# A hybrid decoder layer: the DeltaNet inverse with diagonal blocks of 32 instead of 16, solved on VectorE in groups of four steps

## The chip, the cores and the metric

One Trainium2 chip, one core. The metric is the device time of one execution in microseconds (us). TensorE (PE) multiplies matrices, VectorE (DVE), ScalarE (ACT) and GpSimd (POOL) work element by element, and SyncE (SP) issues the DMA transfers. Each engine runs its own instructions in the order in which the program emits them.

## The reference

One layer of a hybrid decoder on 16 learned meta tokens, 1024 prompt tokens and 8 sample sequences of 8 tokens. One projection of the normalised input (2048 wide) gives the columns of 6 mLSTM heads (A), 6 gated DeltaNet heads (B) and 4 HGRN2 heads (C), each 128 wide, and an output projection follows. The change is in the DeltaNet heads:

```python
def _gdn_segment(q, k, v, g, beta, S0, chunk):
    ...
    A = jnp.where(strict, bc[..., None] * decay * jnp.einsum('nbhtd,nbhsd->nbhts', kc, kc), 0.0)
    M = A + jnp.eye(c, dtype=A.dtype)
    rhs = jnp.concatenate([bc[..., None] * vc, (bc * jnp.exp(G))[..., None] * kc], axis=-1)
    sol = lax.linalg.triangular_solve(M, rhs, left_side=True, lower=True)
    ...
    def step(S, inp):
        q_, k_, U_, Wk_, Aqk_, G_ = inp
        W = U_ - jnp.einsum('bhtd,bhde->bhte', Wk_, S)
        o = jnp.exp(G_)[..., None] * jnp.einsum('bhtd,bhde->bhte', q_, S) + jnp.einsum('bhts,bhse->bhte', Aqk_, W)
        Ge = G_[..., -1:]
        S_new = jnp.exp(Ge)[..., None] * S + jnp.einsum('bhsd,bhse->bhde', k_ * jnp.exp(Ge - G_)[..., None], W)
        return S_new, o
```

In words: per chunk of tokens a unit lower triangular matrix M is inverted (the kernel forms the inverse and multiplies by it), and a state of 128x128 is carried from chunk to chunk.

## The kernel before

The tokens are handled in two halves of 512 prompt tokens; the first half also has the 64 sample and 16 meta tokens, a "small group" of `NT0` = 80. In each half the heads follow in the order gate, C0, B0, A0, B1, A1, C1, B2, A2, B3, A3, C2, B4, A4, B5, A5, C3. For each head `run_group` (line 303) does the projection: a weight block of 128x512 (`wraw`, by DMA) is split by ScalarE into a rounded part `whi` and by VectorE into the rest `wlo = wraw - whi`; three pieces are split ahead and seven loaded ahead. Each quarter of a piece gives three products into `acc` in the second half (`hB`: 512 columns) and six in the first (`hA`: two parts of 288 and 288 or 304 columns). After each quarter `weave.pump()` emits whatever else is due.

What else there is, is written as generators, the streams: the scan of a head (`gdn_scan` for B heads, with others for A and C), its finish, and others. Each stream runs to its next `yield` and gets a due time from a planner's own clock, `ck`: `ck.last + 0.4`, where `ck.last` is the time at which the planner thinks the emitted step is done, or what the code sets it to. A step is emitted when the planner's TensorE time `ck.t["T"]` has passed its due time. Within one queue the streams follow one another, so a scan that comes late makes the next scan late. This sets the order on all engines when the program is written; on the chip, semaphores only make an instruction wait for its operands.

`start_head` (line 1578) begins a head. If two heads are still live it drains the oldest: all its remaining steps are emitted at once, with no projection products between them:

```python
        while len(live) >= 2:
            weave.drain(*live.pop(0)["streams"]())
```

In `gdn_scan` the inverse of the 128x128 matrices of a half's four chunks (and of the small group) is built so. `B` (`Ball`) holds the strictly triangular parts. Diagonal blocks of `SUB` = 16 are solved in `substitute` by 15 steps of two VectorE instructions on `Yc` and `Yt`; each step needs a row of each block of `B` in all partitions of the block, which goes out to a DRAM scratch `db` and comes back broadcast as `Bb`. The result, masked to block diagonal, is `Y`; its transpose `X` is made by TensorE (`px`). Blocks of 16 are joined to 32 by full products `pz` and `pyy` with a mask `zmask` between; `X` is made anew; then blocks of 32 are joined to 64 and of 64 to 128 by small products of the same names. In these names of the trace, `s` and `t` stand for the shared tiles of the main and the small group (`Y`, `X`, `Z`, `vb` and others are such tiles).

Last, the chain of chunks, four rounds a head: `pr` (TensorE, old state `state_B` by keys), then VectorE on `vb` (`s<-pr`), then `pw` (TensorE, inverse by `vb`), ScalarE's copy `Wt`, then `pu` and two `po` (TensorE), VectorE's new `state_B`, and the next `pr`. There is a `yield` after each link, so that projection products can stand between.

The functions that the change touches, with their line numbers in the profile (most instructions are recorded at line 138, in a helper through which every operation goes):

Of the kernel before, what the change touches and what calls it, by code (L numbers as in the profile page):

```python
# [6 lines left out]
F32 = mybir.dt.float32  # L7
F32R = mybir.dt.float32r
U8 = mybir.dt.uint8
BF16 = mybir.dt.bfloat16  # L10
AF = mybir.ActivationFunctionType
ALU = mybir.AluOpType
AX = mybir.AxisListType

P = 128
# [176 lines left out]
def hybrid_step(ctx, tc, i, o):  # L192
    nc = tc.nc
    ck = Clock()
    V, S, G, T = (Engine(ck, n, e) for n, e in (("V", nc.vector), ("S", nc.scalar), ("G", nc.gpsimd), ("T", nc.tensor)))
    DMA = nc.sync.dma_start
    weave = Weave(ck)

    cp = ctx.enter_context(tc.tile_pool(name="cp", bufs=1))
# [24 lines left out]
    ident = cp.tile([P, P], F32, name="ident")  # L224
# [284 lines left out]
    segment_mask(sm0, 1.0, 0.0, True)  # L509

    hmask = {}
    zmask = cp.tile([P, P], BF16, name="zmask")
    m = sq("io", "zm")
    G.memset(m, 0.0)
    v = m.rearrange("p (b x) -> p b x", x=2 * SUB)[:, :, 0:SUB]
    G.memset(v, 1.0)
    G.affine_select(v, v, pattern=[[-2 * SUB, P // (2 * SUB)], [0, SUB]], compare_op=ALU.is_ge, fill=0.0, base=-SUB, channel_multiplier=1)
    G.affine_select(v, v, pattern=[[2 * SUB, P // (2 * SUB)], [0, SUB]], compare_op=ALU.is_ge, fill=0.0, base=2 * SUB - 1, channel_multiplier=-1)
    G.tensor_copy(zmask, m)
# [28 lines left out]
    for r in range(0, P, 32):  # L548
        v = quadmask[r:r + 32]
# [4 lines left out]
    for r in range(0, P, NSAMP):  # L554
        v = rowmask[r:r + NSAMP]
# [39 lines left out]
    rows_dram = [dp.tile([5, HA, h], F32, name=f"rows{h}") for h in (WA, WB)]  # L595
# [178 lines left out]
        return cols_of[half.index][0:g.n, g.idx, kind, h:h + 1].to_broadcast([g.n, g.nt, width])  # L774

    def bc_row(tag, name, half, arr, h):
        t = row(tag, name)[:, 0:half.width]
        DMA(t, rows_dram[half.index][arr, h:h + 1, :].partition_broadcast(P))
        return t


# [363 lines left out]
    def gdn_scan(half, h, ck_, cq, cv, zs, Gb, eG, bb, st):  # L1145
        W = half.width
        gs, main = half.ggroups, half.gmain
        cols = cols_of[half.index]
# [48 lines left out]
        for g, B in zip(gs, Bs):  # L1197
            n = g.n
# [7 lines left out]
        dbf = db.rearrange("j s c t -> j (s c t)")  # L1206
        Bb = []
        for lo, hi, tag in ((0, 6, "s7"), (6, 12, "s9"), (12, 15, "s6")):
            w = C * SUB
            t = sp.tile([P, 512], F32, tag=tag, name="Bb", bufs=1)[:, 0:(hi - lo) * w]  # L1210
            DMA(t, dbf[:, lo * w:hi * w].unsqueeze(1).to_broadcast([P // SUB, SUB, (hi - lo) * w]))
            for x in range(hi - lo):
                Bb.append(t[:, x * w:(x + 1) * w].rearrange("p (c t) -> p c t", t=SUB))
# [7 lines left out]
        Ys, Xs = [], []  # L1221

        def transpose_Y(g, Y, X):
            n = g.n
            px = bank("px")
            for c in range(g.nt):
                T.transpose(g.psum(px, n)[:, c], Y[0:n, c, 0:n], ident[0:n, 0:n])
            S.copy(X[0:n, :, 0:n], g.psum(px, n))

        def substitute():  # L1230
            Yc = sp.tile([P, 5, SUB], F32, tag="Yc", name="Yc", bufs=1)[:, 0:C]
            tmp = sp.tile([P, 5, SUB], F32, tag="Yt", name="Yt", bufs=1)[:, 0:C]
            V.tensor_copy(Yc, subid.unsqueeze(1).to_broadcast([P, C, SUB]))
            for s_ in range(SUB - 1):
                r = slice(s_ + 1, SUB)
                V.tensor_tensor(tmp[:, :, r], Yc[:, :, s_:s_ + 1].to_broadcast([P, C, SUB - 1 - s_]), Bb[s_][:, :, r], op=ALU.mult)
                V.tensor_tensor(Yc[:, :, r], Yc[:, :, r], tmp[:, :, r], op=ALU.subtract)
                if s_ in (4, 9):
                    ck.last = 0.0
                    yield  # L1240
            for g in gs:
                nb = g.n // SUB
                Y = gt("8", g)
                V.tensor_tensor(Y[0:g.n, :, 0:g.n].rearrange("p c (j t) -> p c j t", t=SUB),
                                Yc[0:g.n, g.idx].unsqueeze(2).to_broadcast([g.n, g.nt, nb, SUB]),
                                submask[0:g.n, 0:g.n].rearrange("p (j t) -> p j t", t=SUB).unsqueeze(1).to_broadcast([g.n, g.nt, nb, SUB]),
                                op=ALU.mult)
                Ys.append(Y)

# [83 lines left out]
        next(extra, None)  # L1333
        yield
        transpose_Y(main, Y, X)
        next(extra, None)
        yield
        for hh in (32, 64):
            pz = main.psum(bank("pz"))
            Z = gt("7", main)  # L1340
            blocks = [(slice(b, b + hh), slice(b + hh, b + 2 * hh)) for b in range(0, P, 2 * hh)]
            for l, r in blocks:
                for c in range(NC):
                    T.matmul(pz[r, c, 0:hh], B[l, c, r], X[l, c, l], start=True, stop=True)
            for l, r in blocks:
                S.copy(Z[r, :, 0:hh], pz[r, :, 0:hh])
            yield
            py = main.psum(bank("pyy"))
            for l, r in blocks:
                for c in range(NC):  # L1350
                    T.matmul(py[l, c, 0:hh], Z[r, c, 0:hh], Y[r, c, r], start=True, stop=True)
                    if hh == 32:
                        T.matmul(py[r, c, hh:2 * hh], Y[r, c, r], Z[r, c, 0:hh], start=True, stop=True)
            for l, r in blocks:
                V.tensor_scalar(Y[l, :, r], py[l, :, 0:hh], -1.0, None, op0=ALU.mult)
                if hh == 32:
# [309 lines left out]
    for half, groups in zip(halves, group_lists):  # L1666
# [4 lines left out]
        for n, group in enumerate(groups):  # L1671
# [14 lines left out]
            cols = [col for _, _, col in group]  # L1686
# [48 lines left out]
    for half in halves:  # L1735
        toks = []
        for n, (c0, cnt) in enumerate(half.tiles):
            if half.first and n == 0:
                toks.append((0, NSAMP, xs_flat, ys_flat))
            else:  # L1740
                a = HALF * half.index + c0
# [5 lines left out]
        for cg, some in OUT_UNITS[half.index]:  # L1747
# [28 lines left out]
            for n in some:  # L1776
                _, cnt, xsrc, _ = toks[n]
# [49 lines left out]
```

## Time and profile before

| what | value |
|---|---|
| three runs | 2525.36, 2528.02, 2525.58 us; median 2525.58 |
| the profiled execution | 2525.14 us, span of its instructions 2523.4 us |
| mean granted clock of TensorE | 0.992 |
| TensorE busy | 2456.8 us (97%) |
| VectorE busy | 1427.0 us (57%) |
| ScalarE busy | 1012.3 us (40%) |
| GpSimd busy | 555.0 us (22%) |
| DMA | 350.77 MB |

Rows of a timeline are: start, duration, engine, line, operation, output `<-` inputs, partitions x elements, number of instructions in the row, and in brackets how long the engine had been idle and what it waited for. `acc<-hB,wlo` is a projection product. PEld is the loading of weights into TensorE, beside the products. Rows of waits are: engine and tile, what it waited for, total us, times, longest. Rows of windows are: stretch in us from the start, its length, busy us of PE, PEld, DVE, ACT and POOL with the number of instructions, the granted clock, the DMA share and GB/s.

### The profile page before, as it was taken

What the parts mean: (1) busy time and instruction counts of PE and PEld (TensorE: products, weight loads), DVE (VectorE), ACT (ScalarE), POOL (GpSimd) and SP (SyncE); (2) the same over time, 40 slices, a digit from 0 to 9 for tenths busy, and PEclk for the clock granted to TensorE, in tenths of its full rate; (3) what the DMA queues carried; (4) which work ended last, traced back from release to release, by engine and by line L of the source; (5) the groups of instructions that cost most, each with busy time, mean ns of one, the idle gap of its engine ahead of it and who ended that gap; (6) DMA issues with size and microseconds to landing.
All of it is one profiled execution on the core that took longest, in us unless ns stands there. A gap on an engine that the chain in (4) does not pass through costs nothing.

```text
span 2523.4 us, 43205 instructions
## 1 busy us (share of the span) xinstructions
PE 2456.8 (97%) x15702; PEld 2199.6 (87%) x15702; DVE 1427.0 (57%) x2977; ACT 1012.3 (40%) x2476; POOL 555.0 (22%) x722
## 2 busy tenths in 40 slices
PE   6999999999999999999899999999999999999998
PEld 5899999999999999999687888888888888888886
DVE  7775656765746655556854556554554645323435
ACT  5643434343435333343643434333543334322324
POOL 5331211420314212213320103110320102211201
PEclk9999999999999999999999999999999999999999
DMA  5666655656545454448455445454554548636735
GB/s 129 157 143 147 154 135 122 166 135 133 144 97 143 97 128 115 118 105 225 115 134 122 119 121 130 120 132 100 131 128 111 130 118 264 175 83 195 259 96 184
DMA packets 681041, 350.77 MB, mean 139 GB/s; under 512 B 260004, under 2 KB 622076, under 8 KB 680828
## 3 DMA queue, kind: packets, MB, share of 16 engines
q1 hardware_dynamic: 680828, 348.01, 53.9%
q8 instruction: 123, 2.02, 0.3%
q14 instruction: 90, 0.74, 0.1%
HBM read 285.71 MB, written 62.19 MB: 138 GB/s over the span
## 4 chain that ended last, share of the span: by engine, by line
PE 74%; DMA 6%; issue 6%; DVE 5%; ACT 4%; POOL 3%; SPq 1%; POOLq 0%; DVEq 0%; ACTq 0%
PE acc L138 55%; PE oacc L138 8%; PE pa L138 1%; DVE wlo L138 1%; DMA wraw<-in_w_in_dram 1%; PE po L138 1%; POOL X L138 1%; PE pyy L138 1%; PE pz L138 1%; POOL res L138 1%; ACT whi L138 1%; PE pu L138 1%; ACT L138 1%; PE poh L138 1%; PE nd L138 1%
## 5 line engine op out<-in xcount | busy, mean ns | idle before, releaser
L138 DVE TENSOR_TENSOR wlo<-wraw,whi 128x512 fp32r<-128x512 f32 x720 | 528.4, 738 | 584.9 <-ACT whi L138 566.0
L138 PE MATMUL acc<-hA,whi 128*128 128x288 f32 (+1 forms) x4544 | 823.0, 303 | 11.5 <-ACT whi L138 7.0
L138 ACT CAST whi<-wraw 128x512 fp32r<-128x512 f32 x720 | 441.3, 618 | 879.8 <-PE acc L138 570.2
L138 PE MATMUL acc<-hB,whi 128*128 128x512 f32 x2272 | 723.8, 400 | 4.4 <-ACT whi L138 3.2
L138 PEld LDWEIGHTS acc<-hA,whi 128*128 128x128 f32 x4544 | 678.3, 191 | 17.5 <-ACT whi L138 8.4
L138 PE MATMUL acc<-hA,wlo 128*128 128x288 f32 x2240 | 488.9, 298 | 2.1 <-DVE wlo L138 2.0
L138 PEld LDWEIGHTS acc<-hB,whi 128*128 128x128 f32 x2272 | 411.2, 189 | 84.0 <-ACT whi L138 4.0
L138 PE MATMUL acc<-hB,wlo 128*128 128x512 f32 x1120 | 440.5, 393 | 5.1 <-DVE wlo L138 4.9
L138 PEld LDWEIGHTS acc<-hA,wlo 128*128 128x128 f32 x2240 | 367.1, 190 | 2.9 <-DVE wlo L138 2.9
L138 PE MATMUL oacc<-whi,y 128*128 128x512 f32 x1088 | 344.8, 391 | 1.7 <-ACT whi L138 1.6
L138 PEld LDWEIGHTS acc<-hB,wlo 128*128 128x128 f32 x1120 | 210.6, 188 | 55.9 <-DVE wlo L138 10.4
L138 PEld LDWEIGHTS oacc<-whi,y 128*128 128x128 f32 x1088 | 205.0, 188 | 45.6 <-ACT whi L138 3.4
L138 PE MATMUL oacc<-wlo,y 128*128 128x512 f32 x576 | 225.5, 392 | 2.1 <-DVE wlo L138 2.1
L138 PEld LDWEIGHTS oacc<-wlo,y 128*128 128x128 f32 x576 | 108.6, 189 | 26.1 <-DVE wlo L138 3.9
L138 POOL TENSOR_TENSOR res<-res,fnw 128x512 f32<-128x512 f32 (+1 forms) x34 | 54.3, 1624 | 255.3 <-ACT oscr L138 255.3
L138 POOL TENSOR_TENSOR qd<-qT,emb 128x512 f32<-128x512 f32 x12 | 16.8, 1403 | 355.9 <-PE po L138 355.9
L138 POOL TENSOR_TENSOR y<-y,zs 128x592 fp32r<-128x592 f32 (+1 forms) x32 | 45.5, 1420 | 92.4 <-ACT zs L138 62.8
L138 DVE TENSOR_TENSOR Yt<-Yc,Bb 128x60 f32<-128x60 f32 (+8 forms) x180 | 36.7, 204 | 39.4 <-DMA Bb<-db 34.4
L138 POOL TENSOR_TENSOR hr<-hr,halfneg 128x4 f32<-128x4 f32 (+1 forms) x48 | 47.4, 987 | 46.2 <-DVE hr L138 44.7
L138 POOL TENSOR_TENSOR X<-Ex,hk 128x256 f32<-128x256 f32 (+1 forms) x40 | 38.1, 953 | 87.8 <-PE pa L138 67.9
L138 POOL TENSOR_TENSOR nrm<-nrm,halfneg 128x10 f32<-128x10 f32 x12 | 23.5, 1955 | 122.6 <-DVE nrm L138 122.6
L138 DVE TENSOR_TENSOR Sx<-Sx,lf 128x256 f32<-128x256 f32 (+2 forms) x60 | 36.5, 613 | 20.2 <-ACT Ex L138 19.1
(410 smaller groups left out, 2805.8 us busy)
## 6 DMA issues: line engine op xcount, KB each, us to landing
wraw<-in_w_in_dram SPq DMA_DIRECT2D x564, 256.0 KB
wraw<-in_w_out_dram SPq DMA_DIRECT2D x144, 256.0 KB
y<-y SPq DMA_DIRECT2D x16, 576.0 KB
px<-in_x_prompt_dram SPq DMA_DIRECT2D x32, 256.0 KB
yd<-y SPq DMA_DIRECT2D x128, 64.0 KB
out_dram<-sst SPq DMA_DIRECT2D x16, 512.0 KB
s<-yd SPq DMA_DIRECT2D x32, 256.0 KB
y<-zs SPq DMA_DIRECT2D x32, 256.0 KB
```

The source lines that it names most:

```text
L138: return f(out, *a, **k)
```

## The change

`SUB` becomes 32. The solve takes 31 steps of two VectorE instructions, with a `yield` after every fourth step whose due time is `ck.t["T"] + 3.0` and 0.4; before, there were two `yield`s, due at once. The merge of 16 into 32 with its `zmask`, its `pz` and `pyy` and both `px` transposes go; the transposed blocks `Xc` come from a VectorE transpose of 32x32 blocks, and GpSimd clears `X` and copies two blocks of it. The rows of `B` are written to two scratches (full rows for the upper half of a block, half rows for the lower) and come back into tiles that are free by then: `ck_`, `Gb`, `bb` (rows `Ck`, `Gb`, `bb` in the order below), the old three, and in the first half `cv`. The first step is due 11 us instead of 7 us after the rows are sent for, and what follows the solve 7 us after it. `bc_row` hands out the whole row tile.

```diff
-SUB = 16
+SUB = 32
...
-        db = dp.tile([P // SUB, SUB, C, SUB], F32, name=f"db{half.index}{h}")
-        for j in range(P // SUB):
-            DMA(db[j], Ball[SUB * j:SUB * (j + 1), 0:C, SUB * j:SUB * (j + 1)])
+        nb = P // SUB
+        db = [dp.tile([nb, SUB // 2, C, w], F32, name=f"db{half.index}{h}{w}") for w in (SUB, SUB // 2)]
+        for j in range(nb):
+            a = SUB * j
+            DMA(db[0][j], Ball[a:a + SUB // 2, 0:C, a:a + SUB])
+            DMA(db[1][j], Ball[a + SUB // 2:a + SUB, 0:C, a + SUB // 2:a + SUB])
         Bb = []
-        for lo, hi, tag in ((0, 6, "s7"), (6, 12, "s9"), (12, 15, "s6")):
-            w = C * SUB
-            t = sp.tile([P, 512], F32, tag=tag, name="Bb", bufs=1)[:, 0:(hi - lo) * w]
-            DMA(t, dbf[:, lo * w:hi * w].unsqueeze(1).to_broadcast([P // SUB, SUB, (hi - lo) * w]))
...
-        ready = ck.t["T"] + 7.0
+        def spread_rows(t, cols):
+            at_ = 0
+            while len(Bb) < SUB - 1:
+                x, s_ = divmod(len(Bb), SUB // 2)
+                w = C * (SUB >> x)
+                m = min((cols - at_) // w, SUB // 2 - s_ - x)
+                if m == 0:
+                    return
+                src = db[x].rearrange("j s c t -> j (s c t)")[:, s_ * w:(s_ + m) * w]
+                DMA(t[:, at_:at_ + m * w], src.unsqueeze(1).to_broadcast([nb, SUB, m * w]))
...
+        for t in (ck_, Gb, bb):
+            spread_rows(t, UW)
+        for tag, cols_ in (("s7", 512), ("s9", 512), ("s6", 512), ("Bx", 320)):
+            if len(Bb) < SUB - 1:
+                spread_rows(sp.tile([P, cols_], F32, tag=tag, name="Bb", bufs=1), cols_)
+        ready = ck.t["T"] + 11.0
...
-                if s_ in (4, 9):
-                    ck.last = 0.0
+                if s_ % 4 == 3:
+                    ck.last = ck.t["T"] + 3.0
                     yield
+            V.transpose(Xc.rearrange("p c t -> p (c t)"), Yc[:, main.at:main.at + NC].rearrange("p c t -> p (c t)"))
...
+        spread_rows(cv, UW)
         ck.last = max(ck.last, ready)
         yield
         yield from substitute()
-        ck.last += 8.0
-        yield
-        Xs = [gt("9", main)]
-        transpose_Y(main, Ys[-1], Xs[-1])
+        ck.last = ck.t["T"] + 7.0
+        yield
         extra = first_chain() if half.first else iter(())
-        yield
-        B, Y, X = Bs[-1], Ys[-1], Xs[-1]
-        pz = main.psum(bank("pz"))
-        for c in range(NC):
-            T.matmul(pz[:, c], B[:, c], X[:, c], start=True, stop=True)
-        Z = gt("7", main)
-        V.tensor_tensor(Z, pz, zmask.unsqueeze(1).to_broadcast([P, NC, P]), op=ALU.mult)
-        next(extra, None)
-        yield
-        py = main.psum(bank("pyy"))
-        for c in range(NC):
-            T.matmul(py[:, c], Z[:, c], Y[:, c], start=True, stop=True)
-        V.tensor_tensor(Y, Y, py, op=ALU.subtract)
-        next(extra, None)
-        yield
-        transpose_Y(main, Y, X)
-        next(extra, None)
-        yield
-        for hh in (32, 64):
+        B, Y = Bs[-1], Ys[-1]
+        X = gt("9", main)[0:2 * SUB, :, 0:2 * SUB]
+        G.memset(X, 0.0)
+        for a in (0, SUB):
+            G.tensor_copy(X[a:a + SUB, :, a:a + SUB], Xc[a:a + SUB])
+        for hh in (SUB, 2 * SUB):
...
-                    if hh == 32:
-                        T.matmul(py[r, c, hh:2 * hh], Y[r, c, r], Z[r, c, 0:hh], start=True, stop=True)
+                    if l.stop == SUB:
+                        T.matmul(py[r, c, hh:2 * hh], y, Z[r, c, 0:hh], start=True, stop=True)
```

The later due times move the rest of each B scan. On TensorE, in the first chunk of the chain of head B3 in the second half, before:

```order
L138 MATMUL pr<-state_B_749,knT 128x128
L138 MATMUL acc<-hB_14887,whi 128x512
L138 MATMUL acc<-hB_14888,whi 128x512
L138 MATMUL acc<-hB_14887,wlo 128x512
L138 MATMUL acc<-hB_14676,whi 128x512
L138 MATMUL acc<-hB_14677,whi 128x512
L138 MATMUL acc<-hB_14676,wlo 128x512
L138 MATMUL pw<-s_20176,s_20233 128x128
```

and in the same place now:

```order
L137 MATMUL acc<-hB_14960,wlo 128x512
L137 MATMUL pr<-state_B_742,knT 128x128
L137 MATMUL pw<-s_20301,s_20625 128x128
L137 MATMUL pu_20773<-Wt,s_20183 128x128
L137 MATMUL po_20775<-state_B_742,qd 128x128
L137 MATMUL po_20775<-Wt,s_20282 128x128
L137 MATMUL pr<-state_B_742,knT 128x128
L137 MATMUL pw<-s_20301,s_20625 128x128
L137 MATMUL pu_20789<-Wt,s_20183 128x128
```

The products of projection that stood between `pr` and `pw` are gone from there; the links of this head's four chunks follow one another.

On VectorE, at the start of the solve of the same head, before:

```order
L138 TENSOR_TENSOR wlo<-wraw,whi 128x512
L138 TENSOR_TENSOR Yt<-Yc,Bb 128x4x15
L138 TENSOR_TENSOR Yc<-Yc,Yt 128x4x15
L138 TENSOR_TENSOR wlo<-wraw,whi 128x512
L138 TENSOR_TENSOR Yt<-Yc,Bb 128x4x14
L138 TENSOR_TENSOR Yc<-Yc,Yt 128x4x14
L138 TENSOR_TENSOR Yt<-Yc,Bb 128x4x13
```

and now, after the first group of four steps:

```order
L137 TENSOR_TENSOR Yc<-Yc,Yt 128x4x28
L137 TENSOR_TENSOR wlo<-wraw,whi 128x512
L137 TENSOR_TENSOR Yt<-Yc,Gb 128x4x27
L137 TENSOR_TENSOR Yc<-Yc,Yt 128x4x27
L137 TENSOR_TENSOR Yt<-Yc,Gb 128x4x26
L137 TENSOR_TENSOR Yc<-Yc,Yt 128x4x26
L137 TENSOR_TENSOR Yt<-Yc,Gb 128x4x25
L137 TENSOR_TENSOR Yc<-Yc,Yt 128x4x25
L137 TENSOR_TENSOR Yt<-Yc,Gb 128x4x24
L137 TENSOR_TENSOR Yc<-Yc,Yt 128x4x24
L137 TENSOR_TENSOR wlo<-wraw,whi 128x512
```

The steps are wider (4 chunks by up to 31 columns), and four of them stand between two weight pieces.

On TensorE, in the scan of the mLSTM head A1 in the first half, before:

```order
L138 MATMUL acc<-hA_88,wlo 128x304
L138 MATMUL pot<-ident,tho 80x128
L138 MATMUL pum<-meta_725,kwall 128x137
L138 MATMUL pum<-s_5279,kwall 128x129 x4
L138 MATMUL nd<-sst,spread_723 32x129 x8
L138 MATMUL nd<-t_5268,t_5218 32x129 x2
L138 MATMUL nd<-t_5268,t_5218 16x129
```

and now:

```order
L137 MATMUL pot<-ident,tho 80x128
L137 MATMUL pum<-meta_718,kwall 128x137
L137 MATMUL pum<-s_5436,kwall 128x129 x4
L137 MATMUL acc<-hA_82,whi 128x288
L137 MATMUL acc<-hA_82,whi 128x304
L137 MATMUL acc<-hA_83,whi 128x288
L137 MATMUL acc<-hA_83,whi 128x304
L137 MATMUL acc<-hA_82,wlo 128x288
L137 MATMUL acc<-hA_82,wlo 128x304
L137 MATMUL acc<-hA_84,whi 128x288
```

Twelve projection products now stand between `pum` and `nd`, where none did.

More of the change, by code (lines that the diff above doesn't have):

```diff
@@ L9 @@
 U8 = mybir.dt.uint8
-BF16 = mybir.dt.bfloat16
 AF = mybir.ActivationFunctionType
@@ L511, in hybrid_step @@
     hmask = {}
[L512 to L519, printed above, removed]
     submask = cp.tile([P, P], F32, name="submask")
@@ L776, in bc_row @@
     def bc_row(tag, name, half, arr, h):
-        t = row(tag, name)[:, 0:half.width]
-        DMA(t, rows_dram[half.index][arr, h:h + 1, :].partition_broadcast(P))
+        t = row(tag, name)
+        DMA(t[:, 0:half.width], rows_dram[half.index][arr, h:h + 1, :].partition_broadcast(P))
         return t
@@ L1202, in gdn_scan @@
             V.tensor_tensor(B[0:n, :, 0:n], B[0:n, :, 0:n], g.psum(pk, n), op=ALU.mult)
-        db = dp.tile([P // SUB, SUB, C, SUB], F32, name=f"db{half.index}{h}")
-        for j in range(P // SUB):
-            DMA(db[j], Ball[SUB * j:SUB * (j + 1), 0:C, SUB * j:SUB * (j + 1)])
-        dbf = db.rearrange("j s c t -> j (s c t)")
-        Bb = []
-        for lo, hi, tag in ((0, 6, "s7"), (6, 12, "s9"), (12, 15, "s6")):
-            w = C * SUB
-            t = sp.tile([P, 512], F32, tag=tag, name="Bb", bufs=1)[:, 0:(hi - lo) * w]
-            DMA(t, dbf[:, lo * w:hi * w].unsqueeze(1).to_broadcast([P // SUB, SUB, (hi - lo) * w]))
-            for x in range(hi - lo):
-                Bb.append(t[:, x * w:(x + 1) * w].rearrange("p (c t) -> p c t", t=SUB))
-        ready = ck.t["T"] + 7.0
+        nb = P // SUB
[4 more added lines that the diff above has]
+            DMA(db[1][j], Ball[a + SUB // 2:a + SUB, 0:C, a + SUB // 2:a + SUB])
+        Bb = []
+        def spread_rows(t, cols):
[8 more added lines that the diff above has]
+                DMA(t[:, at_:at_ + m * w], src.unsqueeze(1).to_broadcast([nb, SUB, m * w]))
+                for _ in range(m):
+                    Bb.append(t[:, at_:at_ + w].rearrange("p (c t) -> p c t", c=C))
+                    at_ += w
+        for t in (ck_, Gb, bb):
[4 more added lines that the diff above has]
+        ready = ck.t["T"] + 11.0
         if half.first:
@@ L1220, in gdn_scan @@
         yield
[L1221 to L1228, printed above, removed]
+        Ys = []
+        Yc = sp.tile([P, 5, SUB], F32, tag="Yc", name="Yc", bufs=1)[:, 0:C]
+        Xc = sp.tile([P, NC, SUB], F32, tag="Xc", name="Xc", bufs=1)
         def substitute():
-            Yc = sp.tile([P, 5, SUB], F32, tag="Yc", name="Yc", bufs=1)[:, 0:C]
             tmp = sp.tile([P, 5, SUB], F32, tag="Yt", name="Yt", bufs=1)[:, 0:C]
@@ L1343, in gdn_scan @@
                 for c in range(NC):
-                    T.matmul(pz[r, c, 0:hh], B[l, c, r], X[l, c, l], start=True, stop=True)
+                    T.matmul(pz[r, c, 0:hh], B[l, c, r], Xc[l, c] if hh == SUB else X[:, c], start=True, stop=True)
             for l, r in blocks:
                 S.copy(Z[r, :, 0:hh], pz[r, :, 0:hh])
+            next(extra, None)
             yield
@@ L1350, in gdn_scan @@
                 for c in range(NC):
-                    T.matmul(py[l, c, 0:hh], Z[r, c, 0:hh], Y[r, c, r], start=True, stop=True)
-                    if hh == 32:
-                        T.matmul(py[r, c, hh:2 * hh], Y[r, c, r], Z[r, c, 0:hh], start=True, stop=True)
+                    y = Yc[r, main.at + c] if hh == SUB else Y[r, c, r]
+                    T.matmul(py[l, c, 0:hh], Z[r, c, 0:hh], y, start=True, stop=True)
+                    if l.stop == SUB:
+                        T.matmul(py[r, c, hh:2 * hh], y, Z[r, c, 0:hh], start=True, stop=True)
             for l, r in blocks:
                 V.tensor_scalar(Y[l, :, r], py[l, :, 0:hh], -1.0, None, op0=ALU.mult)
-                if hh == 32:
+                if l.stop == SUB:
                     V.tensor_scalar(X[r, :, l], py[r, :, hh:2 * hh], -1.0, None, op0=ALU.mult)
```

9 lines of the change are left out of this document (5 added, 4 removed).

## The prediction

> **What bounds the kernel now.** I read the page first, then the list of waits, then the timeline of TensorE around the steps that the change touches.
>
> ```profile
> span 2523.4 us, 43205 instructions
> PE 2456.8 (97%) x15702; PEld 2199.6 (87%) x15702; DVE 1427.0 (57%) x2977; ACT 1012.3 (40%) x2476; POOL 555.0 (22%) x722
> ...
> q1 hardware_dynamic: 680828, 348.01, 53.9%
> ...
> PE 74%; DMA 6%; issue 6%; DVE 5%; ACT 4%; POOL 3%; SPq 1%; POOLq 0%; DVEq 0%; ACTq 0%
> ...
> L138 DVE TENSOR_TENSOR wlo<-wraw,whi 128x512 fp32r<-128x512 f32 x720 | 528.4, 738 | 584.9 <-ACT whi L138 566.0
> ...
> L138 ACT CAST whi<-wraw 128x512 fp32r<-128x512 f32 x720 | 441.3, 618 | 879.8 <-PE acc L138 570.2
> ```
>
> TensorE is busy 97% of the span and carries 74% of the chain. VectorE's idle time ends with ScalarE's `whi`, and ScalarE's ends with TensorE's `acc`: the two engines that prepare weight pieces wait for TensorE to use them up. So a microsecond that TensorE wins or loses counts in full, and work elsewhere costs only where it makes TensorE wait. The sum is made against the profiled execution of 2525.1 us, 0.5 us under the median of the three runs; I treat the two as equal.
>
> **Removed TensorE work.** Second half, head B3, TensorE around the merge of 16 into 32:
>
> ```profile
> 2038.75 0.40 PE L138 MATMUL acc<-hB,wlo 128*128 128x512 f32 x1
> 2038.98 1.05 PE L138 MATMUL pz<-s,Ball 128*128 128x128 f32 x8
> ...
> 2040.33 0.39 PE L138 MATMUL acc<-hB,wlo 128*128 128x512 f32 x1
> ...
> 2041.02 0.40 PE L138 MATMUL acc<-hB,wlo 128*128 128x512 f32 x1
> ...
> 2042.61 0.40 PE L138 MATMUL acc<-hB,wlo 128*128 128x512 f32 x1
> ...
> 2043.30 0.39 PE L138 MATMUL acc<-hB,wlo 128*128 128x512 f32 x1
> 2043.53 0.60 PE L138 MATMUL px<-ident,s 128*128 128x128 f32 x4
> ...
> 2044.43 0.39 PE L138 MATMUL acc<-hB,wlo 128*128 128x512 f32 x1
> ```
>
> The durations overlap, so I measure by period: three projection matmuls with nothing between, from `wlo` to `wlo`, take 0.69 us (2040.33 to 2041.02). With `pz` between it is 1.58, with `pyy` 1.59, with the four `px` transposes 1.13. They add 0.89, 0.90 and 0.44 us. The change drops `pz` and `pyy` once and `px` twice per head: 2.67 us, times 12 heads **−32 us**. The four narrow `pyy` matmuls that the merge of 32 loses count as nothing.
>
> **The chain of chunks loses its cover.** In the new order the scans of 11 of the 12 B heads (all but B5 of the second half) reach the drain in `start_head` with their chunk chains still to come, so `pr`, `pw`, `pu`, `po` stand there with no projection between (39 of 44 `pr`→`pw`, 42 `pw`→`pu`, 33 `po`→next `pr`). Before, each is spaced:
>
> ```profile
> 2058.33 0.39 PE L138 MATMUL acc<-hB,wlo 128*128 128x512 f32 x1
> ...
> 2058.56 0.38 PE L138 MATMUL pr<-state_B,knT 128*128 128x128 f32 x2
> ...
> 2058.98 0.35 DVE L138 SCALAR_TENSOR_TENSOR s<-pr,cols,s 128x128 f32<-128x128 f32 x1 [0.79 <-PE pr L138]
> ...
> 2059.25 0.40 PE L138 MATMUL acc<-hB,wlo 128*128 128x512 f32 x1
> ...
> 2059.48 0.40 PE L138 MATMUL pw<-s,s 128*128 128x128 f32 x2
> ...
> 2059.91 0.27 ACT L138 COPY Wt<-pw 128x128 f32<-128x128 f32 x1 [0.48 <-PE pw L138]
> ...
> 2060.18 0.40 PE L138 MATMUL acc<-hB,wlo 128*128 128x512 f32 x1
> ...
> 2060.87 0.40 PE L138 MATMUL acc<-hB,wlo 128*128 128x512 f32 x1
> ...
> 2061.11 0.38 PE L138 MATMUL pu<-Wt,s 128*128 128x128 f32 x2
> 2061.33 0.39 PE L138 MATMUL po<-state_B,qd 128*128 128x128 f32 x2
> ...
> 2061.75 0.35 DVE L138 SCALAR_TENSOR_TENSOR state_B<-state_B,eGb,pu 128x128 f32<-128x128 f32 x1 [1.60 <-PE po L138]
> ...
> 2062.24 0.39 PE L138 MATMUL acc<-hB,wlo 128*128 128x512 f32 x1
> ```
>
> Spaced, `pr` costs 0.92 − 0.69 = 0.23, `pw` 0.93 − 0.69 = 0.24, `pu` with both `po` 1.37 − 0.69 = 0.68: 1.15 us a chunk. Run together, TensorE waits out each link: from a matmul's start to its reader 0.42 or 0.43 us (2058.56→2058.98, 2059.48→2059.91, 2061.33→2061.75), then 0.35 in VectorE or 0.27 in ScalarE, then the way back. One place shows that and the start after a late weight load:
>
> ```profile
> 978.20 0.34 DVE L138 SCALAR_TENSOR_TENSOR state_B<-state_B,eGb,pu 128x128 f32<-128x128 f32 x1
> ...
> 978.60 0.30 PEld L138 LDWEIGHTS pr<-state_B,knT 128*128 128x128 f32 x2 [0.18 <-DVE state_B L138]
> ...
> 979.13 0.35 DVE L138 SCALAR_TENSOR_TENSOR s<-pr,cols,s 128x128 f32<-128x128 f32 x1 [0.58 <-PE pr L138]
> ```
>
> The way back is 0.06 (978.54→978.60), and a link whose weight load had to wait takes 0.53 from the load to the reader. So `pr`→`pw` is 0.53 + 0.35 + 0.06 = 0.94, `pw`→`pu` 0.53 + 0.27 + 0.06 = 0.86. From `pu` to the next `pr` VectorE also waits for the `po` that reads the old state: 0.22 (2061.11→2061.33), 0.42, 0.35 and 0.06, with 0.11 for the late load, 1.16. A chunk takes 2.96 us. Beyond the spaced cost the links are 0.71, 0.62 and 0.48, times 39, 42 and 33: **+70 us**, 6.3 a drain. The bounds: 0.97 us of VectorE and ScalarE plus three matmuls of 0.38 are 2.1 a chunk, +40 in all; half as much again as the sum is +105. I take the sum of links, since each piece of it is in a row of this very chain.
>
> In four of these drains (B1 and B3 of both halves) a C head's key activations stand between the `Wt` copies on ScalarE, elsewhere convolution steps on VectorE. A foreign instruction is of the size of a `whi` (0.62) or `wlo` (0.74). About 1.5 us in each of the four and 0.4 in the seven others: **+9** (0 to 20). The tail, where the last C head's products now follow each other with no projection left: **+4** (0 to 10), sized like four chunk links.
>
> **Relief of the mLSTM scans.** In the first half the drains of before fall on A scans:
>
> ```profile
> PE nd L138 <- DVE s L138: 4.8, 4, 1.8
> ...
> PE pum L138 <- ACT v L138: 2.0, 2, 1.0
> ...
> PE nd L138 <- DVE nsT L138: 1.6, 4, 1.1
> ```
>
> In the new order projection stands between these. The three waits sum to 8.4 us; with the unnamed pauses around them I take **−12** (−8 to −15).
>
> Without the clock: −32 + 70 + 9 + 4 − 12 = **+39**.
>
> **The granted clock.** One place before resembles the run-together chain: transposes, an eviction and products of a first-half B head.
>
> ```profile
> 198.00:204.00 6.00, 3.95 (x23) 3.23 (x22) 3.13 (x6) 3.48 (x10) 4.16 (x5) 0.80 0.58 156
> 204.00:208.00 4.00, 4.00 (x18) 4.00 (x18) 2.09 (x6) 0.00 (x0) 0.11 (x1) 0.50 0.12 30
> ...
> 201.20 0.37 PE L138 MATMUL pkk<-knT 128*80 128x80 f32 x2 [0.93 <-ACT knT L138]
> ...
> 202.30 2.07 PE L138 MATMUL pkk<-knT 128*128 128x128 f32 x8 [0.73 <-ACT knT L138]
> ```
>
> The rows are length, busy time of PE, PEld, DVE, ACT and POOL, then the clock. TensorE was busy 3.95 of 6 us, with waits under a microsecond, and the clock fell: 0.80 in that stretch and 0.50 in the next, although TensorE was busy all of it. Lost are 0.2 × 6 + 0.5 × 4 = 3.2 us. A chunk of the run-together chain has five matmuls of 0.38 us whose issue overlaps, in 2.96 us, no more than that stretch; a drain has four chunks, 11.8 us. I expect the drop in nearly every one: 3.2 us as here to 4.0 (two slowed chunks at about 1.0 more, then 2.0 as in 204:208), taken as 3.7, times 11: **+41**. The bounds are 0 and 11 × 5 = 55.
>
> [...]
>
> **What I cost at nothing, and its cover.** VectorE's longer substitution:
>
> ```profile
> 2026.34 0.22 DVE L138 TENSOR_TENSOR Yt<-Yc,Bb 128x60 f32<-128x60 f32 x1 [3.49 <-DMA Bb<-db]
> ...
> 2034.20 0.17 DVE L138 TENSOR_TENSOR Yt<-Yc,Bb 128x4 f32<-128x4 f32 x1
> ...
> 2034.60 0.69 DVE L138 TENSOR_TENSOR s<-Yc,submask 128x512 f32<-128x512 f32 x1
> ...
> 350.00:390.00 40.00, 40.00 (x359) 39.23 (x358) 27.75 (x70) 14.54 (x37) 4.22 (x7) 1.00 0.55 123
> ```
>
> Thirty instructions take 8.3 us (2026.34 to 2034.60) with some `wlo` pieces between, about 6.5 without: 0.22 each at 32 elements on average. The two `Yt` rows differ by 0.05 over 56 elements, so at 64 on average 0.25, and 62 take 15.5 us; two 128x512 operations of 0.69 go. That is +8 us a head, about +95 on 1427, so 60%. The fullest 40 us that I found near a substitution have 27.75 busy; 8 more still fit. Pieces are split three ahead, and a piece is four periods of 0.69 on TensorE, so the lead is 8 us and no `wlo` should be late. Without that cover each head costs up to the 8 us. The steps yield every four, so at most eight small instructions, 2 us, stand ahead of a `wlo`.
>
> DMA: the rows of B grow by 1.05 MB in each second-half head and 1.31 in each first-half head, 14 MB on 348, two points on 53.9%. SyncE issues three to six more per head behind the same weight loads, which run seven pieces ahead: nothing. The substitution waited 3.49 us for `Bb` and is now due 4 us later; no projection waits for it, but it moves the scan later, which is what brings the chains into the drains. GpSimd's clearing and two copies of `X` fall on an engine busy 22%.
>
> **Rivals.**
> - The clock holds through the chains, which is +39, 2564 us (2545 to 2580). For it: the chains' pauses are each below 0.9 us, shorter than the 0.93 that stood ahead of the drop. [...] Against: the drop itself. This case also covers a drop in only a few drains.
> - VectorE becomes the bound in the B heads: `wlo` late by some 4 of the 8 us in 10 of 12 heads, 2605 + 40 = 2645 or more. For it: 62 instructions of a chain that cannot be spread. Against: 27.75 of 40.
> - Not slower: the drained chains run at the floor of their instructions, 2.1 us a chunk, so +40 in place of +70, the foreign instructions and the tail fall between, the clock holds. −32 − 12 + 40 + 4 = 0, 2525; with links covered by the next head's projection instead, down to 2485. It decides at 4 us a drain: 11 drains at that price pay for the 44 us won. Against it: a reader started 0.42 us after its matmul in every row, later than the matmul's 0.38.
>
> **How the numbers follow.** Clock drops in most drains: 0.58, 2525 + 39 + 41 = 2605, the forecast (own range 2580 to 2630). Clock holds: 0.25, 2564. VectorE late as well: 0.08, over 2630. Not slower: 0.09, of which faster 0.05 and the same 0.04. A measurement of this kernel tells about 0.2%, 5 us, from no change. The range 2545 to 2635 leaves out the last case and most of VectorE's, less than 2 in 10.
>
> **What would show it.** The page after: TensorE's instruction count down, its busy time down while the span is longer, new waits `pw <- DVE s`, `pu <- ACT Wt`, `pr <- DVE state_B` of some 0.4 to 0.7 us in 33 to 42 places each; clock 0.5 in stretches after these chains and a mean below 0.992; VectorE near 60% with few waits of `acc` for `wlo`; the three waits of the mLSTM scans smaller. The forecast fails if the chains cost below 4 us a drain, or if projection stands between the links after all.

## The result and the profile after

| kernel | median of the runs, us | ratio to before, 95% interval | granted clock |
|---|---|---|---|
| before | 2526.2 (4 runs) | | 0.992 |
| changed | 2693.8 (2690.2 to 2696.6, 4 runs) | 1.066 [1.064, 1.068] | 0.958 |

The change costs 168 us. The forecast was 2605, slower by 79, with a range up to 2635: the sign was right, and more than half of the loss was not in the sum. The page of the changed kernel, the same rows as before:

```profile
span 2688.3 us, 42883 instructions
PE 2515.2 (94%) x15318; PEld 2225.5 (83%) x15318; DVE 1512.2 (56%) x3337; ACT 996.2 (37%) x2450; POOL 565.0 (21%) x753
...
q1 hardware_dynamic: 687812, 362.39, 52.3%
...
PE 66%; DMA 13%; DVE 7%; issue 6%; ACT 4%; SPq 3%; POOL 2%; POOLq 0%; DVEq 0%; ACTq 0%
...
L137 ACT CAST whi<-wraw 128x512 fp32r<-128x512 f32 x720 | 441.7, 619 | 1047.3 <-PE acc L137 535.1
```

TensorE's share of the chain fell from 74% to 66%, and that of DMA rose from 6% to 13%. What TensorE waited for, first two rows of the kernel before, then the changed kernel:

```profile
PE acc L138 <- ACT whi L138: 10.2, 8, 3.0
PE acc L138 <- DVE wlo L138: 6.9, 8, 1.4
```

```profile
PE acc L137 <- ACT whi L137: 45.6, 20, 5.6
PE acc L137 <- DVE wlo L137: 36.1, 15, 9.1
PE pw L137 <- DVE s L137: 18.1, 39, 0.8
PE pu L137 <- ACT Wt L137: 17.2, 42, 1.0
...
PE pr L137 <- DVE state_B L137: 5.6, 20, 0.8
```

The last three rows are the links of the chunk chains: the first two of them in the 39 and 42 places that were counted in the new order, the third in 20 of 33. The rows of `acc` were not in the sum: projection itself waits for weight pieces, 82 us in all instead of 17, up to 9.1 us at a time.

To see what each kind of pause costs in all, I took from the trace the time from the start of each projection product to the next, subtracted the median for its width (0.13 or 0.14 us up to 304 columns, 0.23 for 512), and summed the rest by what stands in between (us; "stalls" is where nothing does; the links of the chain include waits of TensorE in or just after the merge where those stand with it):

| kernel | chains of B heads | stalls | merge | mLSTM scans | HGRN2 scans | mean clock |
|---|---|---|---|---|---|---|
| before | 77 | 22 | 55 | 70 | 82 | 0.992 |
| changed | 181 | 89 | 27 | 53 | 87 | 0.958 |
| `before_late` | 184 | 21 | 54 | 53 | 87 | 0.970 |
| `rep8` | 181 | 26 | 27 | 53 | 88 | 0.971 |
| `rep16_early` | 100 | 35 | 27 | 79 | 79 | 0.982 |

The span grew by 165 us. Of that, 104 us lie in the chains, 67 in stalls and 5 in the HGRN2 scans; 28 are won in the merge and 17 in the mLSTM scans. The other 34 or so lie outside these columns; projection products that run slower make up some 15 to 23 of them, depending on how long a delay counts as a stall. Where one stretch holds products of several kinds, the column is a matter of choice, so the figures are good to a few us.

### The profile page after: what moved, and what is told of

It reads as the page before. It is cut to its first block, busy times and chain, and to the rows that moved or that the text cites. A ratio compares the mean times of both kernels' runs of the same rounds, so it can differ in the third digit from the quotient of the medians.

```text
span 2688.3 us, 42883 instructions
## 1 busy us (share of the span) xinstructions
PE 2515.2 (94%) x15318; PEld 2225.5 (83%) x15318; DVE 1512.2 (56%) x3337; ACT 996.2 (37%) x2450; POOL 565.0 (21%) x753
## 4 chain that ended last, share of the span: by engine, by line
PE 66%; DMA 13%; DVE 7%; issue 6%; ACT 4%; SPq 3%; POOL 2%; POOLq 0%; DVEq 0%; ACTq 0%
PE acc L137 47%; PE oacc L137 7%; DMA wraw<-in_w_in_dram 4%; DVE wlo L137 2%; DMA Bb<-db 2%; PE pu L137 1%; PE po L137 1%; PE nd L137 1%; PE pa L137 1%; DMA Ck<-db 1%; ACT whi L137 1%; PE pw L137 1%; POOL res L137 1%; DVE Yt L137 1%; DMA Gb<-db 1%
## 5 line engine op out<-in xcount | busy, mean ns | idle before, releaser
L137 PEld LDWEIGHTS acc<-hA,whi 128*128 128x128 f32 x4544 | 688.0, 193 | 23.7 <-ACT whi L137 14.2
L137 PEld LDWEIGHTS acc<-hB,whi 128*128 128x128 f32 x2272 | 424.8, 192 | 125.1 <-ACT whi L137 38.2
L137 PE MATMUL acc<-hA,wlo 128*128 128x288 f32 x2240 | 495.1, 301 | 32.0 <-DVE wlo L137 31.8
L137 DVE TENSOR_TENSOR Yc<-Yc,Yt 128x100 f32<-128x100 f32 (+55 forms) x372 | 87.6, 236 | 11.2
L137 DVE TENSOR_TENSOR Yt<-Yc,Bb 128x110 f32<-128x110 f32 (+31 forms) x204 | 47.2, 232 | 10.6 <-DMA Bb<-db 4.8
L137 DVE TENSOR_TENSOR s<-s,hr 128x512 f32<-128x512 f32 x32 | 28.2, 882 | 34.8 <-POOL hr L137 34.8
L137 ACT ACTIVATE Ex<-Sx 128x256 f32<-128x256 f32 (+1 forms) x48 | 20.6, 429 | 72.3 <-POOL X L137 39.4
```

What stands on the lines that cost most here:

```text
L137: return f(out, *a, **k)
```

## The experiments

**The order alone.** `before_late` is the kernel before with one number of the planner changed:

```diff
-        ck.last += 8.0
+        ck.last += 28.0
```

> The kernel before, with the one number of the planner after the solve raised from 8 to 28, so that 37, 43 and 32 links of the chunk chains stand together as in the changed kernel (39, 42, 33); blocks of 16, reads and merges unchanged. Theory A (the order alone costs what the trace shows): 2526 + 105 - 17 (mLSTM scans relieved) + 15 (clock after the chains) = about 2629, granted clock near 0.97. Theory B (the chains cost only their links, without the clock): 2526 + 70 - 12 = about 2584.

Measured: 2632.5 us, ratio 1.043 [1.042, 1.045], 107 us over the kernel before. Blocks of 16 and their reads are untouched, so the order by itself brings the whole price of the chains. In the timeline of the changed kernel, head B1 of the second half, such a drain reads:

```profile
1599.91 0.38 PE L137 MATMUL pr<-state_B,knT 128*128 128x128 f32 x2
1600.73 0.49 PE L137 MATMUL pw<-s,s 128*128 128x128 f32 x2 [0.44 <-DVE s L137]
1601.97 0.49 PE L137 MATMUL pu<-Wt,s 128*128 128x128 f32 x2 [0.74 <-ACT Wt L137]
...
1603.12 0.53 PE L137 MATMUL pr<-state_B,knT 128*128 128x128 f32 x2 [0.22 <-DVE state_B L137]
...
1605.80 0.80 PE L137 MATMUL pu<-Wt,s 128*128 128x128 f32 x2 [0.92 <-ACT Wt L137]
...
1607.47 0.79 PE L137 MATMUL pr<-state_B,knT 128*128 128x128 f32 x2
...
1611.52 0.79 PE L137 MATMUL pr<-state_B,knT 128*128 128x128 f32 x2
...
1602.00:1606.00 4.00, 2.42 (x11) 1.71 (x12) 1.36 (x3) 3.93 (x9) 0.00 (x0) 0.68 0.51 133
1606.00:1610.00 4.00, 3.19 (x11) 2.31 (x11) 1.33 (x4) 1.41 (x5) 0.78 (x2) 0.50 0.02 4
```

Before the clock falls no pause is longer than 0.74 us (0.92 comes after), yet from the second chunk on the clock is 0.50 (the number before the DMA share in the last row), the two `pr` products take 0.79 instead of 0.38, and a chunk takes 4.05 us (1607.47 to 1611.52). Over all drained chains of `before_late`, a chunk takes 2.93 us in the median where it runs at full clock and 4.05 at half clock; the changed kernel shows the same two numbers.

**The clock by itself.** `late_fill` adds to `before_late` two products after each link, into a PSUM bank that nobody reads:

```diff
+        pd = bank("pd")
+        def fill():
+            for x in (0, 1):
+                nc.tensor.matmul(pd[:, P * x:P * (x + 1)], ident, ident, start=True, stop=True)
...
+            fill()
```

> The kernel before with the scans moved late (2632 us, granted clock 0.970), plus two extra TensorE products of 128x128 after each link of the chunk chains, into a bank that nobody reads: work that is added in the pauses. Theory A (part of the chain's price is the half clock that its pauses bring, about 3.7 us in each of 11 drains): the clock stays at 1 there, the mean is back to about 0.99, and the time falls in spite of the added work: 2632 - 41 + 3 = about 2594. Theory B (the links alone cost 107 us): the added products cost time or nothing, 2632 to 2645.

Measured: 2615.1 us, ratio 1.035 [1.034, 1.037]. TensorE got more work and the kernel became 17 us faster. The clock and the two waits, first of `before_late`, then of `late_fill`:

```profile
core 0: 2630.7 us, clock 0.970
...
PE pu L138 <- ACT Wt L138: 17.7, 43, 1.3
PE pw L138 <- DVE s L138: 17.6, 37, 0.8
```

```profile
core 0: 2615.1 us, clock 0.988
...
PE pu L138 <- ACT Wt L138: 5.4, 17, 0.4
PE pw L138 <- DVE s L138: 4.2, 11, 0.4
```

No chunk was found at half clock any more, and the mean is 0.988 instead of 0.970, so the drop comes with the pauses, not with the drain's place. The expectation of 2594 was 21 us too low. The filler's own price explains 5 of them: a chunk at full clock takes 3.12 us in the median with it, against 2.93, about 8 us over 44 chunks, where 3 were allowed; the rest isn't traced. The clock is therefore worth at least 17 us here, some 25 with the filler's 8 added back, against the 41 of the sum; its exact share isn't separated.

**Weight pieces late: first remedies.** In the changed kernel, SyncE around the reads for the same head, then the weight piece that TensorE waited for, then a window:

```profile
1540.74 0.53 SPq L238 DMA_DIRECT2D wraw<-in_w_in_dram  x1
1541.45 0.57 SPq L1212 DMA_DIRECT2D Ck<-db  x1
...
1543.22 7.89 SPq L1212 DMA_DIRECT2D Bb<-db  x3
1551.16 14.35 SPq L238 DMA_DIRECT2D wraw<-in_w_in_dram  x5
...
1563.77 0.62 ACT L137 CAST whi<-wraw 128x512 fp32r<-128x512 f32 x1 [14.80 <-DMA wraw<-in_w_in_dram]
...
1564.44 0.79 PE L137 MATMUL acc<-hB,whi 128*128 128x512 f32 x1 [5.07 <-ACT whi L137]
...
1545.00:1553.00 8.00, 8.00 (x37) 6.64 (x36) 3.68 (x12) 1.73 (x3) 0.00 (x0) 1.00 0.25 91
```

For 10.4 us (1540.74 to 1551.16) no weight load is issued, because SyncE issues the six reads, and three of them hold it for 7.89 us. The first load after that is used 12.6 us after its issue. While the reads run, the DMA share is 0.25 of 16 engines, as much as four busy ones, at 91 GB/s. The reads of a head have the pattern [4 blocks][32 partitions][row].

That is a stall of the second half. In the first half the largest four (7.8, 5.1, 8.7 and 9.1 us) come by another way. VectorE waits 9.7 to 13.0 us for another transfer that SyncE issued behind the reads, and `wlo` stands behind that wait in VectorE's queue:

```profile
238.85 0.24 DVE L137 TENSOR_TENSOR Gb<-Gb,am 80x80 f32<-80x80 f32 x1 [13.03 <-DMA Gb<-rows]
...
242.07 0.61 PE L137 MATMUL acc<-hA,wlo 128*128 128x288 f32 x1 [7.75 <-DVE wlo L137]
```

So it isn't weight loads alone that come late behind the reads: `Gb<-rows`, `nm<-rows` and `hblo<-xT`, which SyncE issued after them, did too. The first remedy, `lanes16`, issues each read as four, one for each block:

```diff
-                DMA(t[:, at_:at_ + m * w], src.unsqueeze(1).to_broadcast([nb, SUB, m * w]))
+                for j in range(nb):
+                    DMA(t[SUB * j:SUB * (j + 1), at_:at_ + m * w], src[j:j + 1].to_broadcast([SUB, m * w]))
```

> The changed kernel, but each broadcast read of B's rows is issued as four, one for each block of 32 partitions (24 issues a head instead of 6 to 9 or so; the bytes and the order of everything else stay). Theory A: the 12 stalls in which TensorE waits for weight pieces (66 us in the trace of the changed kernel, 5.5 a head) come from reads whose outermost dimension is 4 and which therefore move on 4 of the 16 DMA engines (DMA share 0.23 to 0.26 and about 100 GB/s while they run), with the weight loads queued behind them. Then they vanish, with the half-clock stretches after them: 2694 - 66 - 15 = about 2613, and the DMA share while the rows are read is above 0.5. Theory B: it is the number of bytes, or SyncE held up by its issues: no better, 2690 to 2740, since issues quadruple.

Measured: 2663.2 us, 1.056 [1.054, 1.057]: between the two theories. SyncE, then ScalarE, VectorE and TensorE at the stall:

```profile
1506.38 0.37 SPq L238 DMA_DIRECT2D wraw<-in_w_in_dram  x1
...
1519.76 5.53 SPq L1213 DMA_DIRECT2D Bb<-db  x12
1525.39 2.04 SPq L238 DMA_DIRECT2D wraw<-in_w_in_dram  x4
...
1528.51 0.62 ACT L137 CAST whi<-wraw 128x512 fp32r<-128x512 f32 x1 [9.13 <-DMA wraw<-in_w_in_dram]
...
1534.76 0.68 DVE L137 TENSOR_TENSOR wlo<-wraw,whi 128x512 fp32r<-128x512 f32 x1
...
1535.50 0.80 PE L137 MATMUL acc<-hB,wlo 128*128 128x512 f32 x1 [5.58 <-DVE wlo L137]
```

The reads are quick now (0.46 us each, 12 in the 5.53 us of the row above), but 8 writes and 24 reads at about half a microsecond each keep SyncE from weight loads for 19 us, and all six second-half heads still stall, for 4.7 to 5.8 us each.

The late load is not what TensorE waits for there: the piece was used 3.1 us after its issue, and its `whi` was ready at 1529.13, before the stall began at 1529.92. TensorE waits for `wlo`, because VectorE had 21 instructions of the solve to run before it (15 to 21 in the six heads). The edit moved more than the reads. TensorE's order is the same but for 8 of its 15318 instructions, but VectorE's order isn't set by the planner alone: between two weight pieces this kernel has up to 47 instructions of the solve, where the changed kernel has 15 at most. So this run answers neither theory cleanly.

What it does show is that a gap of 18 to 19 us between weight loads can just be borne when the loads land 3 us after their issue; of the first-half heads, with gaps of 25 to 29 us, one stalls 5.5 us for its load and the others 1.5 at most. In the changed kernel's second half the gap is only 8.5 to 10.4 us, but the first load lands 12.5 to 14.0 us after its issue. So both the time until a load is issued and the time until it lands behind the reads count. `q_pool` leaves the six reads as they are and lets GpSimd issue them:

```diff
-                DMA(t[:, at_:at_ + m * w], src.unsqueeze(1)...
+                nc.gpsimd.dma_start(t[:, at_:at_ + m * w], src.unsqueeze(1)...
```

> The changed kernel with its 6 to 9 broadcast reads of B's rows a head issued by GpSimd instead of SyncE; same transfers (outermost dimension 4). Theory A2 (the stalls come from SyncE's queue: while it issues 8 writes and the reads, and waits in them, no weight load is issued for 10 to 19 us, by the trace of the changed kernel 1541 to 1551 us and of the one with four reads a block 1506 to 1525): weight loads pass the reads, most of the 66 us of stalls and the clock loss after them go, 2694 - 55 - 12 = about 2627. Theory A (the four DMA engines are busy with the reads whoever issues them): weight loads still wait behind on those four, the stalls stay at 4 us or more a head, 2680 or more.

Measured: 2807.4 us, 1.112 [1.111, 1.114]: in the range of Theory A, but not by its way. Each read follows the one before by 5.3 to 6.5 us, the solve on VectorE waits for them one by one, and the `wlo` pieces wait behind the solve in VectorE's own queue (rows: GpSimd, then waits of TensorE and of VectorE):

```profile
1642.82 0.77 POOL L1212 DMA_DIRECT2D Ck<-db  x1 [8.94 <-DMA db<-Ball]
1649.34 0.68 POOL L1212 DMA_DIRECT2D Gb<-db  x1 [5.75 <-issue]
1654.62 0.68 POOL L1212 DMA_DIRECT2D bb<-db  x1 [4.60 <-issue]
...
PE acc L137 <- DVE wlo L137: 150.6, 60, 7.5
...
DVE Yt L137 <- DMA Bb<-db: 127.1, 43, 4.9
```

It doesn't answer the question it was made for, since a new wait took the place of the old one, but it shows that six reads of this form come no faster when GpSimd issues them (5.3 to 6.5 us from one to the next, where SyncE issued three in 7.89 us).

**Weight pieces late: the cause.** `rep8` and `rep16` keep SyncE's number of issues, the bytes read and the length of the solve between two weight pieces (14 instructions at most), and of the reads they change only the outermost dimension. For that the rows are written twice or four times over (`RC` = 2 or 4; GpSimd first copies the diagonal blocks into a compact tile `Bc`):

```diff
+                DMA(db[x][j].rearrange("r s c t -> s r (c t)"), src.unsqueeze(1).to_broadcast([SUB // 2, RC, src.shape[1]]))
...
-                DMA(t[:, at_:at_ + m * w], src.unsqueeze(1).to_broadcast([nb, SUB, m * w]))
+                DMA(t[:, at_:at_ + m * w], src.unsqueeze(1).to_broadcast([nb * RC, SUB // RC, m * w]))
```

> The changed kernel with the rows of B written four times over into the scratch (GpSimd first copies the diagonal blocks into a compact tile; the number of issues stays 8 writes and 6 to 9 reads a head, all on SyncE), so that a read's outermost dimension is 16 instead of 4; bytes read stay. Theory A+A2 (slow reads on few DMA engines hold SyncE in its issues and the weight loads behind them): the issues of Bb fall from 2.3 us in the median to about 0.6, the stalls for weights go, 2694 - 66 - 15 = about 2613. Theory B (bytes and the number of issues alone): stalls stay, 2680 to 2700.

> The same with two copies, so an outermost dimension of 8, as the reads of the kernel before have. Theory A+A2: most of the way, 2615 to 2640, since 8 engines would move a head's 1.5 MB in about 8 us. Theory B: 2680 to 2700.

Measured: 2599.0 us, 1.029 [1.027, 1.031], and 2598.7 us, 1.029 [1.028, 1.031]. Eight is as good as sixteen, both are faster than expected, and 95 of the 168 us are gone. The `Bb` reads of a whole run (minimum, median and maximum in ns) in the changed kernel, then in `rep8` with SyncE in its last B head, two windows and the two waits of projection:

```profile
L1212 SPq DMA_DIRECT2D Bb<-db x48: 507/2314/4689, 213.7 to 2182.0; - x48
```

```profile
L1220 SPq DMA_DIRECT2D Bb<-db x48: 567/567/1148, 214.5 to 2100.1; - x48
...
2095.74 0.39 SPq L238 DMA_DIRECT2D wraw<-in_w_in_dram  x1
2096.40 0.61 SPq L1220 DMA_DIRECT2D Ck<-db  x1
...
2098.28 2.42 SPq L1220 DMA_DIRECT2D Bb<-db  x3
2100.74 6.82 SPq L238 DMA_DIRECT2D wraw<-in_w_in_dram  x4
...
2097.00:2101.00 4.00, 4.00 (x19) 3.34 (x18) 0.69 (x1) 0.62 (x1) 0.00 (x0) 1.00 0.48 148
2101.00:2105.00 4.00, 4.00 (x19) 3.30 (x18) 3.50 (x12) 1.73 (x3) 0.00 (x0) 1.00 0.75 207
...
PE acc L137 <- ACT whi L137: 14.5, 11, 4.4
...
PE acc L137 <- DVE wlo L137: 6.4, 12, 1.4
```

An issue takes 0.57 instead of 2.31 us in the median, the gap between weight loads is 5.0 instead of 10.4, and the DMA share is 0.48 while the reads are issued and 0.75 at 207 GB/s once weight loads run beside them. With an outermost dimension of 4 the windows show a share of 0.25 of the 16 engines at 91 GB/s, with 8 a share of 0.48 at 148 GB/s. With 16 an issue took 0.60 us in the median. In engines the shares would be about 4 and 8 (0.25 × 16 and 0.48 × 16), which is an estimate: no run shows which engines move a read. The 8 us for a head's 1.5 MB in the expectation of `rep8` are an estimate too, at about twice the 91 GB/s.

**The chains spaced again.** `early` is the changed kernel with shorter waits of the planner; `both` adds the reads of `lanes16`, `both_pool` has those reads issued by GpSimd, `rep16_early` has four copies and 11.0 in the last line:

```diff
-                    ck.last = ck.t["T"] + 3.0
+                    ck.last = ck.t["T"] + 0.3
...
-        ck.last = ck.t["T"] + 7.0
+        ck.last = ck.t["T"] + 9.0
```

> The changed kernel with the waits of the planner shortened (0.3 instead of 3.0 after each group of four steps, and 9.0 instead of 7.0 after the solve): no link of a B chunk chain stands next to another without projection between, while 11 instead of 1 of the mLSTM places stand together; reads unchanged. Theory A: the run-together chains cost 105 us by the trace (links and clock), the stalls for weights are a separate 66: 2694 - 105 - 15 (clock after the chains) + 25 (mLSTM scans) = about 2600, stalls still there. Theory B: the chains are slow because weights are late in any case, so spacing them only moves the wait: over 2650.

> Both edits. Theory A: the two add: 2600 - 66 - 15 = about 2519, near the kernel before (2526): the merge's 29 us of TensorE work saved, less the mLSTM scans run together. Theory B (VectorE's longer solve makes weight pieces late as soon as the solve is not spread out): 2550 or more, with TensorE waiting for wlo in each B head.

> The kernel with both edits (four reads a block, shorter planner waits) with the reads issued by GpSimd. Theory A2: the 46 us of stalls that were left in that kernel (2592 us) go with their clock loss, unless GpSimd's own issuing makes the reads late: 2592 - 46 - 12 = about 2534. If the stalls there come from VectorE (wlo late because of the longer solve), nothing changes: 2585 to 2595.

> Four copies, and the planner's waits shortened (0.3 after each group of four steps, 11.0 after the solve), so that no chunk chain is run together. All terms of the sum together: 2526 - 29 (merge) + 4 (mLSTM scans) + 0 to 25 (the merge still waiting for the solve in some heads) = 2501 to 2526: even with or slightly faster than the kernel before. If the longer solve on VectorE costs TensorE time after all: over 2535.

Measured: `early` 2666.9 us, 1.057 [1.055, 1.059]; `both` 2592.1, 1.027 [1.025, 1.029]; `both_pool` 2580.4, 1.022 [1.021, 1.024]; `rep16_early` 2542.7, 1.007 [1.006, 1.009]. None reached the time that it should have by its first theory. `early` fell short of its 2600 because the merge now came before the solve was done; one row tells it, here of `early`, `both_pool` and `rep16_early`:

```profile
PE pz L137 <- DVE Xc L137: 87.6, 12, 22.1
```

```profile
PE pz L137 <- DVE Xc L137: 56.1, 9, 15.2
```

```profile
PE pz L137 <- DVE Xc L137: 14.7, 7, 3.4
```

The solve ends late, and a scan that isn't moved back waits for it in the open; `early` lies in the range of its Theory B, since much of the wait has moved from the chains to the merge. `both` has 15.3 us of this wait, but its main loss is the one that its Theory B named: TensorE waits 42.8 us for `wlo`, since this kernel too has up to 47 instructions of the solve between two weight pieces. In `both_pool` the stalls, summed as in the table, are as few as in the kernel before (23 us against 22): off SyncE's queue and in quick form, the reads do not hold up weights. That is not the clean answer that `q_pool` couldn't give, since the solve between two pieces is back to 15 at most here. In `rep16_early` the merge's 28 us are won, and the mLSTM scans (79 against 70), the stalls (35 against 22) and the chains, which with the waits for `Xc` are 23 over before, take them back. Its 2542.7 lies where the expectation put a longer solve that costs TensorE time after all. No version tried here is faster than the kernel before.

## Why the prediction was wrong, point by point

- **Removed TensorE work**, forecast −32: −28 by the table. Right. TensorE's busy time rose all the same (2456.8 to 2515.2 us), against the sign that was given for it.
- **The chain of chunks**, forecast 2.96 us a chunk at full clock and about 1.0 more when slowed: 2.93 and 4.05. Right.
- **The granted clock** falls through pauses below a microsecond: right. In the drain shown above it fell after pauses of at most 0.74 us, and `late_fill`, with products in the pauses, brought the mean from 0.970 to 0.988. With the clock held, the other terms of the forecast give 70 + 9 + 4 − 12 = 71; the order alone measured 107.
- **The mLSTM scans**, −12: −17. **Foreign instructions and tail**, +13: the HGRN2 scans took 5 us more, the rest is in the chains.
- **The order together**: 70 + 9 + 4 − 12 + 41 = 112 forecast, 107 measured in `before_late`. How the 107 split between links and clock isn't measured, and what `late_fill` gives for the clock, some 25, isn't 41, so luck may have a part in how close the two sums are. Taking the merge's 28 off 2632 gives 2604; `rep8` measured 2599, and the forecast was 2605.
- **VectorE's longer solve at nothing**: right in `rep8`, with its order. There, with all 62 instructions, TensorE's waits for `wlo` sum to 6.4 us, and `rep8` is 34 us below `before_late`, no less than the merge's saving. The cover that was given, at most eight small instructions ahead of a `wlo`, is no property of the change: the changed kernel has up to 15, and where an order has 35 to 47 of them, as in most heads of `lanes16` and `both`, the solve costs some 5 us in each second-half head. That is the way of the rival that made VectorE the bound, though not in the changed kernel itself. Of the 8 us a head of more VectorE work 7 are in the page (1427 to 1512).
- **The DMA at nothing**: this step failed. "SyncE issues three to six more per head behind the same weight loads, which run seven pieces ahead: nothing" counted the issues and the bytes, but not the form of the transfers. `SUB` = 32 halves the number of blocks, and with it the outermost dimension of the reads, from 8 to 4; while they ran the DMA share was 0.25, SyncE was held in them (7.89 us for three), and what it issued behind them, weight loads and other transfers, landed too late for a lead that the prediction itself put at 8 us of split pieces and four more loaded. Measured price: 2694 − 2599 = 95 us. Of it 63 are the stalls (89 to 26). The other 32 fit the clock, which in the traces of the kernel before and of the changed one is either 1 or 0.50: 2 × (1 − 0.958) × 2688 = 226 us ran at half speed against, if `rep8` too has only these two, 2 × (1 − 0.971) × 2599 = 151, which is at most 37 us of lost TensorE time, less what falls into the stalls themselves. What stays open is how the 95 us divide between SyncE's queue (gaps of 8.5 to 10.4 us between weight loads in the second half, 4.9 to 5.6 in `rep8`) and the transfers behind the reads (12.5 to 14.0 us from the first load's issue to its landing, 9.5 to 11.0 in `rep8` where it shows).

No rival had this mechanism: the one that made weights late put it on VectorE's instructions.

## What to carry to other kernels

When a change alters a tile size, write out the access pattern of each DMA that depends on it and look at its outermost dimension, beside its bytes (here a read held SyncE for 2.31 us in the median with 4 and 0.57 with 8); then look at what stands behind it on the issuing queue and how long that queue's lead is. Work that is cut out of the busiest engine is worth only what it doesn't move: here 28 us of products were saved, and the delay that paid for them pushed 114 dependent links to places with no cover. A pause is charged twice where it also lowers the clock (here a chunk took 4.05 us instead of 2.93), so a run of short dependent links is priced with its slowed form.

## What the hardware showed that was not expected

- A `Bb` read with outermost dimension 4 held SyncE for 2.31 us in the median and up to 4.69, with 8 for 0.57 and up to 1.15; 8 and 16 gave the same time (2598.7 and 2599.0).
- Products that compute nothing of use made the kernel 17 us faster (2632.5 to 2615.1), and the mean granted clock rose from 0.970 to 0.988.
- The quick reads into which `lanes16` split each read held SyncE for 0.46 us each (12 in 5.53 us): 24 of them and 8 writes made a gap of 19 us between weight loads. The loads then landed 3 us after their issue, and the stalls of the second half came from VectorE's order.
